# Four pairs of gate units move out of the first stage of a hybrid encoder layer and run behind it as seven block products each

## The chip, the cores and the metric

The kernel runs on one core of one Trainium2 chip. The metric is the device time of one execution in microseconds (us), the median of several runs. One further execution was taken by the hardware profiler; its rows are in us from the start of its span, with the engines named PE (matmuls), DVE (vector), ACT (scalar), POOL and SP (the engine that issues the DMAs).

## The reference

One encoder layer on 1024 tokens behind 16 meta tokens, width 1024, all in float32. One wide projection of the normed input is cut into the inputs of two branches and two gates:

```python
proj = h @ w_in[l]
(q, k, v, z, b_raw, a_raw, sc_b, sc_c, sc_x, gate_a, gate_b) = jnp.split(proj, SPLIT_POINTS, axis=-1)
o_dn = gated_deltanet_bidir(q, k, v, z, b_raw, a_raw, ...)     # times silu(z) at its end
y_a = o_dn @ w_branch_dn[l]
y_b = (sc_b * depthwise_conv_centred(sc_c * sc_x, sc_conv_w[l])) @ w_branch_sc[l]
merged = jax.nn.sigmoid(gate_a) * y_a + jax.nn.sigmoid(gate_b) * y_b
h_res = h_res + merged @ w_out[l]
gu = h2 @ w_gate_up[l]
h_res = h_res + (silu(gu[..., :D_FF]) * gu[..., D_FF:]) @ w_down[l]
```

The change concerns gate_a, gate_b (1024 columns each, 8 units of 128), z (8 units, one a head) and the short convolution y_b.

## The kernel before

Every product is done on operands that are split into a rounded high part and the low rest (`split`, L98: an ACT copy rounds, a DVE subtraction leaves the rest), as three matmuls: high·high, high·low, low·high. A unit is 128 output columns over 1024 tokens: 2 halves of 512 tokens, 8 steps of the contraction, 3 matmuls each, so 48 matmuls of 512 columns. Its weights come in one DMA of 512 KB into a raw tile (two of them take turns) and are split into `wh` and `wl` (two buffers each). PSUM has eight banks of 512 columns, under the names pm, pe and pd. The normed input lies in SBUF transposed, `hTh` its high part and `al_...` (three tiles) its low part.

**Stage 1** (up to L1393) runs the 24 q, k and v units and, between them, *fill units*: gates, z of the first five heads (`ZH = 5`), and 24 units of the short convolution, in this order (`fill_units`, L958 to 963). Gates go to DRAM as `ta_d` and `tb_d`, z as `z_d`, the convolution as `p_d` (eight tiles, stored by halves out of `rb`, L452), the heads' results as `o_d`. Beside the units four streams run for each head (decay, norm, inverse, scan), whose small matmuls are put between those of the units. The order is written by a planner at build time: it keeps a clock per engine (`T`), adds a cost for each instruction that it places (`pe`, `V`, `A`, `on`), and lets a stream go on when PE's clock has reached the time at which the stream's data should be ready. In `g_norm` a loop over the nine chunks multiplies the decay matrices PQ with products of k and q (L602, L641); `on("dve", 500)` stands ahead of it, and `freed_at` says when a bank is free again. The instructions of stage 1 stay in the planner's order on every engine.

**Behind stage 1** the framework's scheduler orders the instructions of each engine, once, at build time. A new pool takes the place of stage 1's SBUF memory, with the tiles b0 to b3 (16 KB a partition each), mA and mB, four s4, w2, and two more raw tiles. Whatever is written there first waits until stage 1's last reads of that memory are done, the stores of `p_d` among them. Then:

- the three z units left (L1411 to 1418), into mB;
- `px`: the eight `p_d` tiles are loaded into s4 tiles and split into b0 to b3 (L1422 to 1426);
- `w_bsc`: eight units on px, times tanh-form gate B, into mA and mB (`mg`); `gated(h)` (L1429) loads o_d, multiplies it by silu(z) and splits it into `ox`;
- `w_bdn`: eight units on ox, times gate A, added; then w_out with the residual and the second norm;
- the feed-forward part: 22 units of two weight blocks of 128 columns each (L1561 is their matmul), and the down projection.

The feed-forward part uses seven block products instead of eight. With weights A11, A12 (one unit's two halves of the contraction), A21, A22 (the other's), and the moving operand's blocks B (halves of the contraction by halves of the tokens), it forms S1 = A21 + A22, S3 = A11 − A21, S2 = S1 − A11, S4 = A12 − S2 (`sums`, L1535) and T1 = B12 − B11, T2 = B22 − T1, T3 = B22 − B12, T4 = B21 − T2 once, and multiplies A11·B11, A12·B21, S2·T2, S1·T1, S3·T3, S4·B22, A22·T4. A product (`product`, L1555) is 4 steps × 3 = 12 matmuls, so a pair takes 84 where two units take 96.

Of the kernel before, what the change touches and what calls it, by code (L numbers as in the profile page):

```python
# [28 lines left out]
ZH = 5  # L29
EPS = 1e-6  # L30
NEG = -1e30

OQ, OK, OV, OZ, OBA, OSB, OSC, OSX, OGA, OGB = (
    0, 1024, 2048, 3072, 4096, 4128, 5152, 6176, 7200, 8224)


def unit(col):

    return (col if col < OBA else col - 32) // P
# [8 lines left out]
def encoder_layer(ctx: ExitStack, tc: tile.TileContext, x, meta, norm1_w, w_in, w_ba,  # L48
                  dn_conv_w, A_log, dt_bias, dn_norm_w, sc_conv_w, w_bdn, w_bsc,
                  w_out, norm2_w, w_gu, w_down, final_w, out):  # L50
    nc = tc.nc
    x, out = x[0], out[0]
# [7 lines left out]
    dr = ctx.enter_context(tc.tile_pool(name="dr", bufs=1, space=DRAM))  # L60
# [16 lines left out]
    def pss():  # L77
        return ps.tile([P, 512], F32, tag="d", name=uid("pd"), bufs=3)
# [3 lines left out]
    def psz():  # L82

        rot["i"] += 1
        return (psm, psd, psm, psd, psd)[rot["i"] % 5]()
# [8 lines left out]
    mm = nc.tensor.matmul  # L94
# [4 lines left out]
    def split(hi, lo, src):  # L99
        nc.scalar.copy(hi, src)  # L100
        nc.vector.tensor_tensor(out=lo, in0=src, in1=hi.bitcast(F32), op=ALU.subtract)  # L101
# [75 lines left out]
    def sub(out, a, b):  # L177
        nc.vector.tensor_tensor(out=out, in0=a, in1=b, op=ALU.subtract)
# [67 lines left out]
    low_tiles = low([LP])  # L246
# [18 lines left out]
    def on(e, ns, ready=0.0):  # L265

        T[e] = max(T[e], ready, T["pe"]) + ns
        return T[e] + TOPE
# [5 lines left out]
    def V(n, kind=0):  # L274
        return on("dve", (68 + 1.042 * n, 130 + 1.042 * n, 130 + 0.52 * n)[kind])
# [210 lines left out]
    B = lambda b: slice(32 * b, 32 * b + 32)  # L486
# [62 lines left out]
    def g_norm(h, st_):  # L549
# [79 lines left out]
        for c in range(NC):  # L629
            while not nxt or c not in st_["exp"]:  # L630
                ask()
                yield T["pe"] + 100
            pk, t = nxt.pop(0)
            while T["pe"] < max(t, st_["exp"][c]):
                ask()
                yield T["pe"] + 100
            for d in range(2):
                nc.vector.scalar_tensor_tensor(out=NP[:, c, d], in0=pk[:, 0:P], scalar=cc[:, c, d:d + 1],
                                               in1=PQ[:, c, d], op0=ALU.mult, op1=ALU.mult)
                V(P, 1)  # L640
            nc.vector.tensor_tensor(out=PQ[:, c], in0=pk[:, P:2 * P].unsqueeze(1).broadcast_to([P, 2, P]), in1=PQ[:, c],  # L641
                                    op=ALU.mult)
# [140 lines left out]
    def g_scan(h, st_):  # L783
# [159 lines left out]
        for c4 in range(2):  # L943
            oT = NP[:, 4 * c4:4 * c4 + 4, 1 - c4]
            pt = newbank()
            for c in range(4):
# [452 lines left out]
    def big(tag, shape, dtype=F32R):  # L1399
        return tp.tile(shape, dtype, tag=tag, name=uid(tag))  # L1400

    def four(tag):

        tiles = [big(f"b{i}", [P, 4, SEQ]) for i in range(4)]
        return [[tiles[2 * i + k // 4][:, k % 4] for k in range(KT)] for i in range(2)]

    px = four("p")
    mg = [big("mA", [P, 4, SEQ], F32), big("mB", [P, 4, SEQ], F32)]
    szs = {}
    for h in range(ZH, H):  # L1410
        w = wload(w_in, unit(OZ + h * P))  # L1411
        sz = szs[h] = mg[1][:, h - ZH]
        for i in range(2):
            po = psany()
            dense(po, w, hx, C0 + META + 512 * i, 512)
            sl = slice(512 * i, 512 * i + 512)
            nc.scalar.activation(sz[:, sl], po, AF.Tanh, scale=0.5)
            nc.vector.scalar_tensor_tensor(out=sz[:, sl], in0=sz[:, sl], scalar=1.0, in1=po, op0=ALU.add, op1=ALU.mult)

    warm2 = keep.tile([P, 1], F32, name="warm2")  # L1420
    nc.scalar.activation(warm2, szs[H - 1][:, SEQ - 1:SEQ], AF.Silu)
    for j in range(KT):  # L1422
        pr = s4(SEQ)
        nc.sync.dma_start(pr, p_d[j])
        split(px[0][j], px[1][j], pr)
    raw_slots.extend((tp, f"raw{i}") for i in range(2))
    ox = (ap_.tile([P, KT, SEQ], F32R, tag="ah", name="oh"), eighths(low([SEQ])))

    def gated(h):  # L1429

        ot = s4(SEQ)
        nc.sync.dma_start(ot, o_d[h])
        if h not in szs:
            szs[h] = s4(SEQ)
            nc.sync.dma_start(szs[h], z_d[h])
        nc.vector.scalar_tensor_tensor(out=ot, in0=ot, scalar=cols[:, 24:25], in1=szs[h], op0=ALU.mult, op1=ALU.mult)
        split(ox[0][:, h], ox[1][h], ot)

    gated_order = [*range(ZH, H), *range(ZH)]
    for j in range(KT):  # L1440
        w = wload(w_bsc, j)
        if j == 0:
            for h in range(ZH, H):
                gated(gated_order.pop(0))
# [78 lines left out]
    def stationary1(j):  # L1523
# [11 lines left out]
    def sums(rg, ru, s2, s4_, s3, s1):  # L1535
        g0, g1, u0, u1 = rg[:, 0:4], rg[:, 4:8], ru[:, 0:4], ru[:, 4:8]
        nc.vector.tensor_tensor(out=s1, in0=u0, in1=u1, op=ALU.add)
        sub(s3, g0, u0)
        sub(s2, s1, g0)
        sub(s4_, g1, s2)  # L1540

    def stationary2(j, ru, sa, sb, A_):

        for i, r in enumerate((sa, sb)):
            sh, sl = (s_hl[j % 2][:, m, i] for m in range(2))
            split(sh, sl, r)
            for x, n in enumerate((("S2", "S4"), ("S3", "S1"))[i]):
                A_[n] = sh[:, 4 * x:4 * x + 4], sl[:, 4 * x:4 * x + 4]

    def block22(j, ru, A_):  # L1550
        uh, ul = (u_hl[j % 2][:, i] for i in range(2))
        split(uh, ul, ru[:, 4:8])
        A_["A22"] = uh, ul

    def product(po, a, b, add_to=False):  # L1555

        (ah, al), (bh, bl) = a, mov[b]
        for k in range(4):
            bhk, blk = (m[k] if isinstance(m, list) else m[:, k] for m in (bh, bl))
            for x, y, i in ((ah, bhk, 0), (ah, blk, 1), (al, bhk, 2)):  # L1560
                mm(po, x[:, k], y, start=k + i == 0 and not add_to, stop=k == 3 and i == 2, skip_group_check=add_to)  # L1561

    add = lambda out, a, b: nc.vector.tensor_tensor(out=out, in0=a, in1=b, op=ALU.add)  # L1563
    mul = lambda out, a, b: nc.vector.tensor_tensor(out=out, in0=a, in1=b, op=ALU.mult)

    def part1(w, p1, sg):

# [253 lines left out]
```

## Time and profile before

| | us |
|---|---|
| median of 3 runs (2011.54 to 2012.34) | 2011.95 |
| the profiled execution | 2009.93 |
| its span | 2008.2 |
| mean granted clock of PE | 0.997 |
| PE, DVE, ACT, POOL busy | 1988.4, 1341.5, 815.6, 108.6 |
| last matmul of stage 1 ends, about | 1062.4 |
| first matmul of w_bsc | 1095.05 |

How to read it: in the rows, "out<-in" are the tiles written and read by the program's names, x the number of instructions, and in brackets the idle time of the engine before the row with what ended it. A row of a wait list gives the total, the number and the longest. A back-to-back matmul shows 0.39 us although the next starts 0.227 us later, since their ends overlap; the distance of starts is the pace.

### The profile page before, as it was taken

The page shows a single profiled execution, that of the slowest core. Times are in us where ns is not written, and L with a number is a line of the kernel's source. Part 1 is how long each engine was busy: PE and PEld are TensorE (multiplying, and loading weights), DVE is VectorE, ACT ScalarE, POOL GpSimd, SP SyncE. Part 2 cuts the span into 40 slices and gives each one's busy share as a digit, 9 for nine tenths or more (in the row PEclk, how much of TensorE's full clock was granted, in tenths as well). Part 3 has the DMA queues.
Part 4 walks back from the last instruction along what each step waited for, and adds up shares of the span by engine and source line. Part 5 has one row for each costly group of instructions (what it writes and reads, how often), then busy time and mean ns, then how long its engine had stood idle before and what let it go on. Part 6 is the DMA issues. An engine that isn't in the chain of part 4 may idle for free.

```text
span 2008.2 us, 31913 instructions
## 1 busy us (share of the span) xinstructions
PE 1988.4 (99%) x12059; PEld 1730.0 (86%) x12059; DVE 1341.5 (67%) x2966; ACT 815.6 (41%) x1945; POOL 108.6 (5%) x407
## 2 busy tenths in 40 slices
PE   9999999999999999999999999999999999999998
PEld 8998889898989899999998888887888888888887
DVE  6887687887888788845335434468866666646575
ACT  6463464646555536333113211224423333334344
POOL 2011101010101020100000000000000000000000
PEclk9999999999999999999999999999999999999999
DMA  3122222323222212221216633122666345477654
GB/s 134 64 90 87 87 90 61 104 69 91 69 80 74 69 57 72 59 75 53 73 54 241 216 130 116 50 98 101 245 225 222 137 150 187 159 271 244 195 172 167
DMA packets 131409, 247.85 MB, mean 123 GB/s; under 512 B 45045, under 2 KB 54694, under 8 KB 128823
## 3 DMA queue, kind: packets, MB, share of 16 engines
q1 hardware_dynamic: 130679, 244.77, 36.9%
q8 instruction: 94, 1.54, 0.3%
q10 hardware_dynamic: 576, 1.05, 0.1%
q14 instruction: 60, 0.49, 0.1%
HBM read 179.10 MB, written 66.67 MB: 122 GB/s over the span
## 4 chain that ended last, share of the span: by engine, by line
PE 90%; DVE 5%; ACT 2%; DMA 2%; issue 1%; SPq 0%; POOL 0%; DVEq 0%; ACTq 0%; POOLq 0%
PE pm L340 35%; PE pd L1561 11%; PE pe L1561 5%; PE pm L1561 3%; PE pe L133 1%; PE pe L135 1%; PE pe L134 1%; PE pd L901 1%; PE pe L602 1%; PE pd L133 1%; PE pd L135 1%; PE pd L134 1%; PE pd L880 1%; PE pe L1728 1%; PE pe L1727 1%; PE pe L1729 1%
## 5 line engine op out<-in xcount | busy, mean ns | idle before, releaser
L340 PE MATMUL pm<-hTh,wh 128*128 128x512 f32 (+4 forms) x1424 | 496.6, 353 | 0.4 <-ACT hTh L1101 0.2
L340 PE MATMUL pm<-al,wh 128*128 128x512 f32 (+4 forms) x1424 | 495.1, 352 | 0.0
L340 PE MATMUL pm<-hTh,wl 128*128 128x512 f32 (+4 forms) x1424 | 494.5, 352 | 0.0
L340 PEld LDWEIGHTS pm<-hTh,wh 128*128 128x128 f32 x1424 | 267.0, 188 | 18.0 <-ACT hTh L1101 0.8
L340 PEld LDWEIGHTS pm<-hTh,wl 128*128 128x128 f32 x1424 | 267.1, 188 | 17.1 <-issue 0.8
L340 PEld LDWEIGHTS pm<-al,wh 128*128 128x128 f32 x1424 | 267.1, 188 | 16.5 <-issue 0.4
L101 DVE TENSOR_TENSOR al<-raw,ring_h 128x1024 fp32r<-128x1024 f32 x73 | 88.5, 1221 | 65.6 <-ACT ring_h L100 64.8
L988 DVE TENSOR_TENSOR wl<-raw,wh 128x512 fp32r<-128x512 f32 x134 | 90.6, 687 | 58.2 <-ACT wh L991 57.9
L100 ACT CAST ring_h<-raw 128x1024 fp32r<-128x1024 f32 x73 | 76.7, 1053 | 107.0 <-PE pd L1729 33.9
L362 DVE SCALAR_TENSOR_TENSOR kq<-ra,wc,kq 128x520 f32<-128x520 f32 x128 | 96.5, 754 | 6.2 <-ACT kq L392 5.3
L991 ACT CAST wh<-raw 128x512 fp32r<-128x512 f32 x134 | 79.5, 621 | 30.4 <-PE pm L340 26.7
L100 ACT CAST wh<-raw 128x1024 fp32r<-128x1024 f32 x43 | 45.1, 1050 | 99.2 <-PE pe L134 35.3
L887 ACT ACTIVATE w<-pd,small 128x128 f32<-128x128 f32 x128 | 39.9, 364 | 100.7 <-PE pd L880 100.4
L495 DVE TENSOR_TENSOR tm<-fP,fN 128x135 f32<-128x135 f32 (+23 forms) x248 | 71.9, 290 | 4.6 <-DVE fP L499 0.2
L499 DVE TENSOR_TENSOR fP<-fP,tm 128x135 f32<-128x135 f32 (+23 forms) x248 | 71.2, 287 | 4.9
L1563 DVE TENSOR_TENSOR b<-pd,b 128x512 f32<-128x512 f32 x22 | 15.2, 690 | 68.9 <-PE pd L1561 68.9
L1664 ACT ACTIVATE b<-b 128x512 f32<-128x512 f32 x22 | 13.9, 632 | 112.8 <-DVE b L1563 112.8
L101 DVE TENSOR_TENSOR wl<-raw,wh 128x1024 fp32r<-128x1024 f32 x43 | 52.4, 1218 | 4.9 <-ACT wh L100 4.8
L1561 PE MATMUL pd<-b_hl,wh 128*128 128x512 f32 x176 | 54.4, 390 | 0.0
L854 ACT ACTIVATE jk<-NP 128x128 f32<-128x128 f32 x64 | 19.9, 311 | 82.6 <-DVE NP L850 81.5
L545 ACT ACTIVATE PQ<-PQ,negG 128x128 f32<-128x128 f32 x128 | 43.6, 394 | 20.2 <-DVE PQ L540 20.1
L874 DVE SCALAR_TENSOR_TENSOR r<-pd,negEG,vS 128x128 f32<-128x128 f32 x120 | 36.7, 345 | 21.8 <-PE pd L864 21.5
(523 smaller groups left out, 4419.5 us busy)
## 6 DMA issues: line engine op xcount, KB each, us to landing
raw<-in_w_in_dram SPq DMA_DIRECT2D x72, 512.0 KB
raw<-in_w_gate_up_dram SPq DMA_DIRECT2D x44, 512.0 KB
sums<-in_w_down_dram SPq DMA_DIRECT2D x22, 512.0 KB
t_d<-sums SPq DMA_DIRECT2D x11, 1024.0 KB
raw<-s_d SPq DMA_DIRECT2D x44, 256.0 KB
raw<-t_d SPq DMA_DIRECT2D x44, 256.0 KB
act_d<-b SPq DMA_DIRECT2D x43, 256.0 KB
raw<-act_d SPq DMA_DIRECT2D x33, 256.0 KB
```

Of the source, the lines that this page charges most:

```text
L100: nc.scalar.copy(hi, src)
L101: nc.vector.tensor_tensor(out=lo, in0=src, in1=hi.bitcast(F32), op=ALU.subtract)
L133: mm(po[:m, :n], wh[:, k, :m], xhk[:, t0:t0 + n], start=(k == 0), stop=False)
L134: mm(po[:m, :n], wh[:, k, :m], xlk[:, t0:t0 + n], start=False, stop=False)
L340: mm(po[:, :n], ww[:, k], f(k)[:, t0:t0 + n], start=i == 0, stop=i == 3 * KT - 1)
L362: nc.vector.scalar_tensor_tensor(out=acc, in0=raw[:, h0 + t:h0 + t + hn], scalar=wc[:, t, col:col + 1], in1=acc, op0=ALU.mult, op1=ALU.add)
L495: nc.vector.tensor_tensor(out=tv, in0=fP[:, 0:r, j:j + 1].broadcast_to([P, r, n]), in1=fN[:, j:j + 1, j + 1:32].broadcast_to([P, r, n]), o ...
L499: nc.vector.tensor_tensor(out=fP[:, 0:r, j + 1:32], in0=fP[:, 0:r, j + 1:32], in1=tv, op=ALU.subtract)
L545: nc.scalar.activation(PQ[:, c, d], PQ[:, c, d], AF.Exp, bias=negG2[:, c, hd:hd + 1])
L988: nc.vector.tensor_tensor(out=u[1][1][:, k], in0=u[2][:, k], in1=u[1][0][:, k].bitcast(F32), op=ALU.subtract)
L991: nc.scalar.copy(u[1][0][:, k], u[2][:, k])
L1561: mm(po, x[:, k], y, start=k + i == 0 and not add_to, stop=k == 3 and i == 2, skip_group_check=add_to)
```

## The change

`GH = 4`: only gates 0 to 3 stay fill units; the eight units of gates 4 to 7 are made by four calls of `pair(n, j)` behind the z units, each with gate A and gate B of one j as its two units, in seven products. For these `moving_sums()` forms T1 to T4 of the normed input into b0 to b3, with mA and mB as scratch (all passes on DVE but the rounding). z of heads 5 to 7 goes to DRAM like the others and is loaded again in `gated`, which takes one head a step from head 0. `px` comes behind the pairs, with `mg`: p_d 0 to 3 are loaded into mA, 4 and 5 into s4 tiles, 6 and 7 into raw tiles. In the planner, 900 instead of 500 is added to DVE's clock ahead of the decay loop, and each chunk gets 110 more and a bank that counts as free 100 later. `sums`, `stationary2`, `product` and the two short helpers move up unchanged. In all PE has 48 matmuls of 512 columns less.

```diff
+GH = 4
-    z_d = [dr.tile([P, SEQ], F32, name=f"z_d{i}") for i in range(ZH)]
+    z_d = [dr.tile([P, SEQ], F32, name=f"z_d{i}") for i in range(H)]
-        on("dve", 500)
+        on("dve", 900)
-            freed_at.append(V(2 * P))
+            on("dve", 110)
+            freed_at.append(V(2 * P) + 100)
-                   for j in range(8) for off, d_ in ((OGA, ta_d), (OGB, tb_d))]
+                   for j in range(GH) for off, d_ in ((OGA, ta_d), (OGB, tb_d))]
-    px = four("p")
-    mg = [big("mA", [P, 4, SEQ], F32), big("mB", [P, 4, SEQ], F32)]
-    szs = {}
+    def moving_sums():
+
+        c = [slice(C0 + META + 512 * i, C0 + META + 512 * i + 512) for i in range(2)]
...
+        x, y = (big(g, [P, 2, 4, 512], F32) for g in ("mA", "mB"))
+        t1, t2, t3, d_ = x[:, 0], x[:, 1], y[:, 0], y[:, 1]
+        a, b = slice(0, 2), slice(2, 4)
+        sub(t1, h0[1], h0[0])
+        sub(d_, l0[1], l0[0])
+        add(t1, t1, d_)
+        split(*mov["T1"], t1)
+        sub(t2, h1[1], t1)
...
+        split(*mov["T4"], t1)
+
+    raw_slots.extend((tp, f"raw{i}") for i in range(2))
+    weights_z = [wload(w_in, unit(OZ + ZH * P))]
+    moving_sums()
     for h in range(ZH, H):
-        w = wload(w_in, unit(OZ + h * P))
-        sz = szs[h] = mg[1][:, h - ZH]
+        w = weights_z.pop() if weights_z else wload(w_in, unit(OZ + h * P))
+        sz = s4(SEQ)
...
+        nc.sync.dma_start(z_d[h], sz)
+    def pair(n, j):
+
+        last = j == KT - 1
+        s_hl[n % 2] = big(("mB", "mA")[n % 2], [P, 2, 2, KT, P])
...
+        if not last:
+            product(bank, A_["S2"], "T2", True)
+            nc.scalar.copy(o1[:, right], bank)
+            product(bank2, A_["S1"], "T1")
+            nc.scalar.copy(o2[:, right], bank2)
+            product(bank, A_["S3"], "T3", True)
...
+            product(bank2, A_["S4"], "B22", True)
+            add(o1[:, right], bank2, o1[:, right])
+            half_turn(o1[:, right])
+        nc.sync.dma_start(ta_d[j], o1)
+        nc.sync.dma_start(tb_d[j], o2)
+        return o1
+
+    for n, j in enumerate(range(GH, KT)):
+        o1 = pair(n, j)
-    nc.scalar.activation(warm2, szs[H - 1][:, SEQ - 1:SEQ], AF.Silu)
+    nc.scalar.activation(warm2, o1[:, SEQ - 1:SEQ], AF.Silu)
+    mg = [big("mA", [P, 4, SEQ], F32), big("mB", [P, 4, SEQ], F32)]
+    px = four("p")
     for j in range(KT):
-        pr = s4(SEQ)
+        pr = mg[0][:, j] if j < 4 else s4(SEQ) if j < 6 else rawtile([P, SEQ])
         nc.sync.dma_start(pr, p_d[j])
         split(px[0][j], px[1][j], pr)
-    raw_slots.extend((tp, f"raw{i}") for i in range(2))
-        if h not in szs:
-            szs[h] = s4(SEQ)
-            nc.sync.dma_start(szs[h], z_d[h])
+        sz = s4(SEQ)
+        nc.sync.dma_start(sz, z_d[h])
```

What the scheduler makes of it, at three places (numbers of tiles are running numbers; a row is one instruction, or several where an x stands).

DVE before, from the end of stage 1: the last short-conv rows (rb), the low part of the second z unit's weights (wl_12903), px splits (b), the third's (wl_12963).

```order
L450 TENSOR_TENSOR rb_12781<-pm_12802,rb_12781 128x512
L101 TENSOR_TENSOR wl_12903<-raw_12904,wh_12902 128x1024
L1418 SCALAR_TENSOR_TENSOR mB_12841<-mB_12841,pm_12848 128x512
L101 TENSOR_TENSOR b_2143_12838<-s_2162_13024,b_2141_12836 128x1024
L101 TENSOR_TENSOR b_2143_12838<-s_2163_13028,b_2141_12836 128x1024
L101 TENSOR_TENSOR b_2143_12838<-s_2164_13032,b_2141_12836 128x1024
L1418 SCALAR_TENSOR_TENSOR mB_12841<-mB_12841,pe_12875 128x512
L101 TENSOR_TENSOR wl_12963<-raw_12964,wh_12962 128x1024
```

DVE after, at the same place: the low part of the second z unit's weights is wl_12417, then come the T sums in mA and mB and their low parts in b.

```order
L451 TENSOR_TENSOR rb_12272<-pm_12293,rb_12272 128x512
L102 TENSOR_TENSOR wl_12417<-raw_12418,wh_12416 128x1024
L179 TENSOR_TENSOR mA_12337<-hTh 128x2048
L179 TENSOR_TENSOR mB_12338<-al_124 128x2048
L179 TENSOR_TENSOR mB_12338<-hTh 128x2048
L1409 TENSOR_TENSOR mA_12337<-mA_12337,mB_12338 128x2048
L1486 SCALAR_TENSOR_TENSOR s_2094_12360<-s_2094_12360,pm_12361 128x512
L179 TENSOR_TENSOR mA_12337<-hTh,mA_12337 128x2048
L102 TENSOR_TENSOR b_2088_12333<-mA_12337,b_2088_12333 128x2048
L1409 TENSOR_TENSOR mA_12337<-mA_12337,al_125 128x1024
L1409 TENSOR_TENSOR mA_12337<-mA_12337,al_126 128x1024
```

And the end of that piece, behind three rows that are left out, up to the low part of the third z unit's weights (wl_12479); s_2094 and s_2100 are z tiles.

```order
L1409 TENSOR_TENSOR mB_12338<-mB_12338 128x2048
L179 TENSOR_TENSOR mA_12337<-hTh,mA_12337 128x2048
L102 TENSOR_TENSOR b_2090_12335<-mB_12338,b_2090_12335 128x2048
L1409 TENSOR_TENSOR mA_12337<-mA_12337,al_125 128x1024
L1409 TENSOR_TENSOR mA_12337<-mA_12337,al_126 128x1024
L1486 SCALAR_TENSOR_TENSOR s_2094_12360<-s_2094_12360,pe_12388 128x512
L1486 SCALAR_TENSOR_TENSOR s_2100_12422<-s_2100_12422,pe_12423 128x512
L1486 SCALAR_TENSOR_TENSOR s_2100_12422<-s_2100_12422,pe_12450 128x512
L102 TENSOR_TENSOR wl_12479<-raw_12480,wh_12478 128x1024
L102 TENSOR_TENSOR b_2091_12336<-mA_12337,b_2091_12336 128x2048
```

Between the second and the third unit's low parts lay three px passes of 1024 columns and two z passes of 512; now ten passes of 2048, six of 1024 and four of 512 stand there.

PE after, at the third z unit (wh_12478, wl_12479) and the first products of the first pair (wh_12542):

```order
L136 MATMUL pe_12450<-hTh,wl_12417 128x512
L134 MATMUL pd_12485<-hTh,wh_12478 128x512
L135 MATMUL pd_12485<-al_124,wh_12478 128x512
L134 MATMUL pd_12512<-hTh,wh_12478 128x512
L135 MATMUL pd_12512<-al_124,wh_12478 128x512
L1440 MATMUL pd_12550<-hTh,wh_12542 128x512
L1440 MATMUL pd_12550<-al_124,wh_12542 128x512
L1440 MATMUL pm_12566<-hTh,wh_12542 128x512
L1440 MATMUL pm_12566<-al_125,wh_12542 128x512
L136 MATMUL pd_12485<-hTh,wl_12479 128x512
```

Two matmuls for each half of the third z unit and four of the pair were drawn ahead of the first row that reads wl_12479.

SP before, behind the last stores of p_d: the px loads follow at once, into s4 tiles (s).

```order
L452 DMA p_d_82<-rb_12769 128x512
L452 DMA p_d_82<-rb_12781 128x512
L118 DMA raw_13062<-in_w_branch_sc_dram 128x1024
L1424 DMA s_2162_13024<-p_d_75 128x1024
L1424 DMA s_2163_13028<-p_d_76 128x1024
L1424 DMA s_2164_13032<-p_d_77 128x1024
L1424 DMA s_2165_13036<-p_d_78 128x1024
L1424 DMA s_2166_13040<-p_d_79 128x1024
```

SP after, at the px loads: s_2147 is the last pair's gate A, mA_13027 the first half of `mg` on the memory of the last pair's S blocks.

```order
L1577 DMA s_2168_13071<-o_d_107 128x1024
L119 DMA raw_13208<-in_w_branch_sc_dram 128x1024
L1579 DMA s_2169_13073<-z_d_99 128x1024
L1558 DMA tb_d_98<-s_2148_12911 128x1024
L119 DMA raw_13275<-in_w_branch_sc_dram 128x1024
L1570 DMA mA_13027<-p_d_75 128x1024
L1557 DMA ta_d_90<-s_2147_12910 128x1024
L1570 DMA mA_13027<-p_d_76 128x1024
L1570 DMA mA_13027<-p_d_77 128x1024
L1570 DMA mA_13027<-p_d_78 128x1024
```

The loads of p_d 0 to 3 (p_d_75 to 78) stand behind the pairs, and three of them behind the store of ta_d_90.

PE after, from the last pair's last product (mA_12903 are its S blocks) to the first w_bsc units (wh_13065):

```order
L1440 MATMUL pe_12925<-hTh,mA_12903 128x512
L134 MATMUL pd_13080<-b_2154_13029,wh_13065 128x512
L134 MATMUL pm_13106<-b_2154_13029,wh_13065 128x512
L135 MATMUL pd_13080<-b_2156_13031,wh_13065 128x512
L136 MATMUL pd_13080<-b_2154_13029,wl_13066 128x512
L135 MATMUL pm_13106<-b_2156_13031,wh_13065 128x512
L136 MATMUL pm_13106<-b_2154_13029,wl_13066 128x512
L134 MATMUL pm_13147<-b_2154_13029,wh_13139 128x512
L134 MATMUL pd_13080<-b_2154_13029,wh_13065 128x512
```

The first rows of w_bsc, on the high parts of p_d 0 to 3 (b_2154), now stand right behind the last row that reads mA_12903.

More of the change, by code (lines that the diff above doesn't have):

```diff
@@ L1405, in four, with sums @@
         return [[tiles[2 * i + k // 4][:, k % 4] for k in range(KT)] for i in range(2)]
-    px = four("p")
-    mg = [big("mA", [P, 4, SEQ], F32), big("mB", [P, 4, SEQ], F32)]
-    szs = {}
+    add = lambda out, a, b: nc.vector.tensor_tensor(out=out, in0=a, in1=b, op=ALU.add)
+    mul = lambda out, a, b: nc.vector.tensor_tensor(out=out, in0=a, in1=b, op=ALU.mult)
+    s_hl, u_hl = [None, None], [None, None]
+    mov = {}
+    def sums(rg, ru, s2, s4_, s3, s1):
+        g0, g1, u0, u1 = rg[:, 0:4], rg[:, 4:8], ru[:, 0:4], ru[:, 4:8]
+        nc.vector.tensor_tensor(out=s1, in0=u0, in1=u1, op=ALU.add)
+        sub(s3, g0, u0)
+        sub(s2, s1, g0)
+        sub(s4_, g1, s2)
@@ new lines, in stationary2, with block22, product @@
+    def stationary2(j, ru, sa, sb, A_):
+        for i, r in enumerate((sa, sb)):
+            sh, sl = (s_hl[j % 2][:, m, i] for m in range(2))
+            split(sh, sl, r)
+            for x, n in enumerate((("S2", "S4"), ("S3", "S1"))[i]):
+                A_[n] = sh[:, 4 * x:4 * x + 4], sl[:, 4 * x:4 * x + 4]
+    def block22(j, ru, A_):
+        uh, ul = (u_hl[j % 2][:, i] for i in range(2))
+        split(uh, ul, ru[:, 4:8])
+        A_["A22"] = uh, ul
+    def product(po, a, b, add_to=False):
+        (ah, al), (bh, bl) = a, mov[b]
+        for k in range(4):
+            bhk, blk = (m[k] if isinstance(m, list) else m[:, k] for m in (bh, bl))
+            for x, y, i in ((ah, bhk, 0), (ah, blk, 1), (al, bhk, 2)):
+                mm(po, x[:, k], y, start=k + i == 0 and not add_to, stop=k == 3 and i == 2, skip_group_check=add_to)
@@ new lines, in moving_sums @@
+    def moving_sums():
+        c = [slice(C0 + META + 512 * i, C0 + META + 512 * i + 512) for i in range(2)]
+        f = lambda m: m.bitcast(F32)
+        h0, h1 = ([f(hx[0][:, 4 * i:4 * i + 4, cc]) for cc in c] for i in range(2))
+        l0, l1, l2 = ([f(t[:, :, cc]) for cc in c] for t in low_tiles)
+        for i in range(2):
+            for j in range(2):
+                mov[f"B{i + 1}{j + 1}"] = hx[0][:, 4 * i:4 * i + 4, c[j]], [hx[1][4 * i + k][:, c[j]] for k in range(4)]
+        for i, n in enumerate(("T1", "T2", "T3", "T4")):
+            t = big(f"b{i}", [P, 2, 4, 512])
+            mov[n] = t[:, 0], t[:, 1]
+        x, y = (big(g, [P, 2, 4, 512], F32) for g in ("mA", "mB"))
[6 more added lines that the diff above has]
+        sub(t2, h1[1], t1)
+        add(t2[:, a], t2[:, a], l1[1])
+        add(t2[:, b], t2[:, b], l2[1])
+        split(*mov["T2"], t2)
+        sub(t3, h1[1], h0[1])
+        sub(d_[:, a], l1[1], l0[1][:, a])
+        sub(d_[:, b], l2[1], l0[1][:, b])
+        add(t3, t3, d_)
+        split(*mov["T3"], t3)
+        sub(t1, h1[0], t2)
+        add(t1[:, a], t1[:, a], l1[0])
+        add(t1[:, b], t1[:, b], l2[0])
+        split(*mov["T4"], t1)
@@ L1442, in encoder_layer @@
         if j == 0:
-            for h in range(ZH, H):
-                gated(gated_order.pop(0))
+            gated(gated_order.pop(0))
         tb = s4(SEQ)
@@ L1533, in stationary1 @@
         return rg, ru, {"A11": (gh[:, 0:4], gl[:, 0:4]), "A12": (gh[:, 4:8], gl[:, 4:8])}, (gh, gl)
[L1535 to L1564, printed above, removed]
     def part1(w, p1, sg):
```

58 lines of the change are left out of this document (56 added, 2 removed).

## The prediction

> **What bounds the kernel now.** I read the page first: span, busy shares, the strip of forty slices, and the summary of the chain that ended last.
>
> ```profile
> span 2008.2 us, 31913 instructions
> PE 1988.4 (99%) x12059; PEld 1730.0 (86%) x12059; DVE 1341.5 (67%) x2966; ACT 815.6 (41%) x1945; POOL 108.6 (5%) x407
> PE   9999999999999999999999999999999999999998
> PEclk9999999999999999999999999999999999999999
> PE 90%; DVE 5%; ACT 2%; DMA 2%; issue 1%; SPq 0%; POOL 0%; DVEq 0%; ACTq 0%; POOLq 0%
> ```
>
> PE is busy in every slice at an undivided clock, and 90% of the chain is PE. So a matmul taken away is worth its pace, and everything else counts only where PE has to wait for it. Next I read what PE waited for in the whole run.
>
> ```profile
> PE pd L1561 <- ACT b L100: 2.6, 1, 2.6
> PE pe L602 <- DVE PQ L641: 2.5, 2, 2.4
> PE pd L97 <- POOL eps L1759: 1.6, 1, 1.6
> ```
>
> These are the three longest, under 7 us together: one at the start of the feed-forward part (L1561), one in the decay loop (L602), one at the end. A new wait of some us would therefore stand out, and nothing in the kernel makes it up again. Third, the pace of a matmul, from the chain in time, and the stretches on which the terms below rest (columns: PE busy, weight loads, DVE, ACT, POOL, granted clock, DMA share, GB/s).
>
> ```profile
> 1417.17 2.72 PE pe L1561 x12
> 1419.89 2.72 PE pd L1561 x12
> ...
> 942.00:1062.40 120.40, 120.40 (x683) 112.77 (x682) 39.50 (x64) 16.32 (x32) 0.20 (x2) 1.00 0.21 68
> 1062.40:1095.00 32.60, 32.60 (x145) 27.02 (x144) 19.09 (x19) 13.81 (x16) 0.00 (x0) 1.00 0.83 291
> 1394.00:1402.00 8.00, 7.10 (x22) 5.09 (x23) 6.97 (x9) 2.73 (x5) 0.00 (x0) 0.79 0.46 164
> 684.00:692.00 8.00, 7.49 (x148) 6.39 (x148) 7.31 (x22) 2.48 (x7) 0.00 (x0) 0.79 0.15 60
> 1400.00:1790.00 390.00, 389.74 (x1717) 321.70 (x1716) 260.92 (x354) 137.41 (x187) 0.00 (x0) 1.00 0.56 195
> 362.00:662.00 300.00, 299.11 (x2404) 268.57 (x2403) 244.69 (x736) 164.22 (x530) 34.97 (x141) 1.00 0.25 78
> ```
>
> One product is 12 matmuls of 512 columns in 2.72 us, so one costs 2.72/12 = 0.2267 us. The stretch 942 to 1062.4 is the tail of stage 1, where nothing but fill units runs. 1062.4 to 1095 is the three z units (144 matmuls × 0.2267 = 32.6), with px prepared beside them and no idle PE.
>
> **The change part by part.** Times below count from t = 0, the end of stage 1's last matmul.
>
> *Fewer matmuls: −10.9 us.* Eight gate units of 48 matmuls leave stage 1 (384 × 0.2267 = 87.0 us) and return as four pairs of 7 × 12 = 84. Each pair saves 12: 48 × 0.2267 = 10.9. Moving 336 matmuls is worth nothing by itself, because PE is full on both sides. The feed-forward stretch 1400 to 1790 runs the same form of product with PE busy 389.74 of 390.00, with its own sums and splits beside it; I take the pairs at that pace once they run.
>
> *The T sums ahead of the third z unit's weights: +12.4 us.* In the new DVE order ten passes of 128x2048, six of 128x1024 and four of 128x512 stand between the second z unit's low part and the third's (wl_12479). DVE works in order. The prices:
>
> ```profile
> 1382.20 4.48 DVE L101 TENSOR_TENSOR b<-al,b 128x2048 fp32r<-128x2048 f32 x2
> ...
> 1078.25 3.49 DVE L101 TENSOR_TENSOR b<-s,b 128x1024 fp32r<-128x1024 f32 x3
> ...
> 1076.52 0.68 DVE L1418 SCALAR_TENSOR_TENSOR mB<-mB,pe 128x512 f32<-128x512 f32 x1
> 1077.11 1.22 DVE L101 TENSOR_TENSOR wl<-raw,wh 128x1024 fp32r<-128x1024 f32 x1
> ```
>
> Back to back that is 4.48/2 = 2.24, 3.49/3 = 1.16 and 1077.11 − 1076.52 = 0.59 us. The queue is 10 × 2.24 + 6 × 1.16 + 4 × 0.59 = 31.7 us, and the low part itself 1.2. When can it begin? Its first pass writes mA, on stage 1's memory, and must wait until the last short-conv rows have been stored.
>
> ```profile
> 1062.41 0.39 PE L133 MATMUL pm<-hTh,wh 128*128 128x512 f32 x1
> ...
> 1065.48 11.46 SPq L1424 DMA_DIRECT2D s<-p_d  x7
> ```
>
> Before, stage 1 ended at 1062.41, and the first load that needs the same stores was issued at 1065.48: t = 3.1. So wl_12479 is whole at 3.1 + 31.7 + 1.2 = 36.0. Until then PE has two z units and eight matmuls that were drawn forward: (96 + 8) × 0.2267 = 23.6. It stands idle for 12.4 us. ACT's rounding casts keep just ahead (1.9 us each for 2048 columns, below) and should add nothing. Bounds: 10, if DVE starts at t = 1 and some passes are shorter, to 15, if a cast or a store is late twice. Behind this the pairs' own weight sums stand in the same queue; DVE gains on PE from there, since a pair asks for 84 × 0.2267 = 19.0 us of PE and the feed-forward stretch keeps DVE at 260.92/390.00 = 67% for the same kind of work.
>
> *px behind the pairs: +6.5 us.* Before, the eight p_d loads and splits lay beside the z units. Now p_d 0 to 3 go into mA, which holds the last pair's S blocks, and its last product (S4B22) reads them to the end of the pairs, call it E. Loads 2 to 4 stand on SP's queue behind the store of ta_d[7], which waits for the last eviction (about E + 2.2, an add and a tanh as below). What a p_d load then costs:
>
> ```profile
> 1070.26 1.05 ACT L100 CAST b<-s 128x1024 fp32r<-128x1024 f32 x1 [1.56 <-DMA s<-p_d]
> 1071.75 1.05 ACT L100 CAST b<-s 128x1024 fp32r<-128x1024 f32 x1 [0.43 <-DMA s<-p_d]
> 1074.29 1.05 ACT L100 CAST b<-s 128x1024 fp32r<-128x1024 f32 x1 [1.49 <-DMA s<-p_d]
> ...
> 1082.25 1.22 DVE L101 TENSOR_TENSOR b<-s,b 128x1024 fp32r<-128x1024 f32 x1
> ...
> 1098.47 1.28 ACT L1421 ACT_TABLE_LOAD   x1
> ...
> 1392.33 1.90 ACT L100 CAST b<-al 128x2048 fp32r<-128x2048 f32 x1 [5.46 <-DVE al L227]
> 1394.28 0.50 PE L1561 MATMUL pd<-b,w 128*128 128x512 f32 x1 [2.60 <-ACT b L100]
> ```
>
> The load issued at 1065.48 was cast at 1070.26, 4.8 us later, and the next two 1.5 and 2.5 us after that. So the first cast begins about E + 4.8 (behind the activation table's 1.28 us, hidden by then), its low part is done 1.05 + 1.22 later at E + 7.1, and the fourth, issued from E + 2.7, about E + 12 to 14. Meanwhile PE can run the blocks of p_d 4 to 7 only: 26 matmuls stand in its order before it is bound to the late four, 26 × 0.2267 = 5.9 us. The wait is 12.4 − 5.9 = 6.5 us, between 5 and 8 by the same rows (landing 1.5 us earlier or later).
>
> *The clock behind each idle time: +3.0 us.* After the waits of 2.4 and 2.6 us the granted clock over the next 8 us is 0.79 (rows 684 and 1394 above), a price of 0.21 × 8 = 1.7 us. Two new waits make 3.4; in px part of it is hidden under the remaining waits, so I take 3.0, from 0 (all hidden) to 5 (a wait in several pieces). The Trainium skill, page "TensorE: Matmul & The Clock Gate", section "HAM oscillation — how this bites in real kernels", gives a rule: "no PE-idle gaps >~3.4µs". By it the waits of 2.4 and 2.6 us should not have touched the clock; the rows 684 and 1394 show 0.79 behind both, so the measurement decides, and by the rule only the decay wait's part of the next term would be smaller by 1.7 us.
>
> *Stage 1: −2.0 us.* The larger numbers in the decay loop only move matmuls: L602 is asked for later, so that its wait can vanish.
>
> ```profile
> 681.79 0.34 PE L340 MATMUL pm<-hTh,wl 128*128 128x384 f32 x1
> 684.51 0.67 PE L602 MATMUL pe<-kq 128*128 128x256 f32 x2 [2.38 <-DVE PQ L641]
> ```
>
> That is worth 2.5 us and its 1.7 of clock: 4.2 at best. Against it, the short-conv units now run inside the head streams instead of in the pure tail (683 fill matmuls stood behind the last scan, 99 now), and DVE is already 244.69/300 = 82% busy from 362 to 662, where PE nevertheless lost under 1 us. One or two more waits like that of 681.8 would cost 4.2 each. Between −4.2 and +5 I take −2.0, nearer to the row that shows how little a full DVE has cost.
>
> *z 5 to 7 through DRAM, reordered gating:* nothing; three stores and three loads more of 512 KB, before stages with a DMA share of 0.56 to 0.83 that PE did not notice. Without that cover one late load would cost about the 4.8 us above.
>
> **Sum:** −10.9 + 12.4 + 6.5 + 3.0 − 2.0 = +9.0 us. The profiled execution took 2009.93 us (span 2008.2), so it would come to 2018.9. The median of the runs before, 2011.95, lies 2.0 above, so the forecast is 2021 us. About 0.2%, 4 us, is what a measurement of this kernel can tell from no change.
>
> **The rivals.**
> - *The low part of the third z unit comes in time* (other side). If DVE ran the T passes in the gaps of stage 1's tail, or the load of the weights let it go first, the queue ahead of it would be under 23.6 − 3.1 − 1.2 = 19.3 us instead of 31.7, and the 12.4 and 1.7 go: 2021 − 14.1 = 2006.9. For it: DVE is only 39.50/120.40 busy in the tail. Against it: the order of the queue is fixed, and mA is not free before the stores. With px hidden as well it would be about 1998.7. Chance 0.13.
> - *Only half of it.* One wait is a good deal smaller, or stage 1 gains its 4.2 and px waits 5 with no clock loss: 2021 − 6 to 8 = about 2014, within no change. Chance 0.17.
> - *The fuller streams run dry.* With shorts inside the streams DVE comes late at L602 or in the scans, two or three times at 4.2 us: 2021 + 2 + 8.4 = about 2031. For it: DVE at 82%. Against it: under 1 us lost there in 300. Chance 0.10.
> - *The change does not save what it says.* The pairs' products read a bank that is still being added to by the last one and so wait about one product each, 4 × 2.72 = 10.9, which eats the whole saving: 2032. Against it: the feed-forward stretch with the same chain of products waits nowhere. Chance 0.05.
>
> **How the numbers follow.** The forecast, both waits within their bounds, has 0.55 (about 2014 to 2028). Faster (under 2007.9): the first rival less its upper edge, and a little of the second, 0.13. Same (2007.9 to 2016.0): the second rival, the first's edge and the forecast's lower one, 0.20. Slower: the rest, 0.67. The range of 8 in 10 takes in the lower rivals down to 2007 and the bounds upwards, 2.6 for the first wait, 1.5 for the second, 2 for the clock and 3 of the 7 of stage 1, 2021 + 9.1 = 2030: 2007 to 2030.
>
> **What would show it.** Right: PE idle 10 to 15 us about 24 us behind stage 1's last matmul, ended by DVE's low part of a z weight; a second idle time of 5 to 8 us in the first w_bsc unit, ended by a low part of p_d; clock below 0.9 behind both; PE without waits between the pairs' products; 48 matmuls fewer; the wait of L602 gone or small. Wrong: if the third z unit starts without a wait the first rival holds; if waits at L602 or in the scans add up to over 5 us, the third; if PE waits inside the pairs, the fourth.

## The result and the profile after

The changed kernel takes 2020.68 us (median of 6 runs, 2018.89 to 2023.88), the kernel before 2011.6 us (median of 6 runs beside it, 2009.31 to 2012.34). The ratio is 1.0053, 95% interval 1.0043 to 1.0063; it is an estimate of its own and not the quotient of the two medians, which is 1.0045. So the change makes the kernel slower, by 9.1 us between the medians and by 10.7 by the ratio, where 9.0 had been forecast (2021).

The page of the profiled execution, with the strips that stood full before:

```profile
span 2022.2 us, 31878 instructions
PE 1980.3 (98%) x12011; PEld 1724.5 (85%) x12011; DVE 1398.3 (69%) x3013; ACT 838.1 (41%) x1961; POOL 109.2 (5%) x407
PE   9999999999999999999798999999999999999998
PEclk9999999999999999999899999999999999999999
PE 88%; DVE 6%; DMA 3%; ACT 2%; issue 1%; SPq 0%; DVEq 0%; ACTq 0%
```

The count of PE instructions is down by 48 (12059 to 12011). In PE's strip two slices, 20 and 22, are no longer full, and the clock of slice 20 is down too. A slice is 2022.2/40 = 50.6 us, so these are 961 to 1011 and 1062 to 1112 us: the third z unit and the first w_bsc unit. The list of PE's waits names what ended them:

```profile
PE pd L136 <- DVE wl L102: 11.5, 1, 11.5
PE pd L134 <- ACT b L101: 6.0, 1, 6.0
PE pd L1440 <- DVE b L1409: 3.3, 2, 2.7
PE pd L1440 <- ACT b L101: 2.6, 1, 2.6
PE pe L603 <- DVE PQ L642: 1.9, 1, 1.9
```

The two at the top are new; the 2.6 is the old wait at the start of the feed-forward part; L603 stands for the old L602. PE in time, first at the z units, then at w_bsc (a row's bracket holds the idle time before it and what ended it):

```profile
970.85 0.39 PE L134 MATMUL pm<-hTh,wh 128*128 128x512 f32 x1
...
994.54 0.39 PE L1440 MATMUL pm<-al,wh 128*128 128x512 f32 x1
1006.41 0.79 PE L136 MATMUL pd<-hTh,wl 128*128 128x512 f32 x1 [11.48 <-DVE wl L102]
1007.00 0.63 PE L134 MATMUL pd<-hTh,wh 128*128 128x512 f32 x1
1007.43 0.63 PE L135 MATMUL pd<-al,wh 128*128 128x512 f32 x1
...
1012.06 0.40 PE L134 MATMUL pd<-hTh,wh 128*128 128x512 f32 x1
...
1094.32 0.39 PE L1440 MATMUL pe<-hTh,mA 128*128 128x512 f32 x1
1100.72 0.80 PE L134 MATMUL pd<-b,wh 128*128 128x512 f32 x1 [6.01 <-ACT b L101]
...
1104.22 0.40 PE L134 MATMUL pd<-b,wh 128*128 128x512 f32 x1
```

Stage 1 ends at 970.85, where 1062.4 − 87.0 = 975.4 would be the old place less the eight units: it gained 4.5 us. The first wait ends 35.6 us later. Behind it the matmuls start 0.43 us apart instead of 0.227, about half the pace: 13 of them take 1012.06 − 1006.41 = 5.65 us instead of 13 × 0.2267 = 2.95, which is 2.7 us of clock; behind the second wait 7 take 3.50 instead of 1.59, another 1.9.

This profiled execution took 2023.88 us, the longest of the six, and is 14.0 longer in span than the one before. The parts seen so far are −10.9 + 11.5 + 2.7 + 6.0 + 1.9 − 4.5 = +6.7. Another 2.7 and its clock, some 1.7, belong to a wait in the feed-forward part that the next profiles show shorter (last section); the rest, 2.9, lies at several places, none of them above 1 us.

### The profile page after: what moved, and what is told of

Same layout as the page of the kernel before. It is cut to its first block, busy times and chain, and to the rows that moved or that the text cites. A ratio compares the mean times of both kernels' runs of the same rounds, so it can differ in the third digit from the quotient of the medians.

```text
span 2022.2 us, 31878 instructions
## 1 busy us (share of the span) xinstructions
PE 1980.3 (98%) x12011; PEld 1724.5 (85%) x12011; DVE 1398.3 (69%) x3013; ACT 838.1 (41%) x1961; POOL 109.2 (5%) x407
## 4 chain that ended last, share of the span: by engine, by line
PE 88%; DVE 6%; DMA 3%; ACT 2%; issue 1%; SPq 0%; DVEq 0%; ACTq 0%
PE pm L341 32%; PE pd L1440 11%; PE pe L1440 5%; PE pm L1440 3%; PE pd L903 1%; PE pd L882 1%; PE pd L866 1%; PE pe L603 1%; PE pd L136 1%; PE pd L135 1%; PE pd L134 1%; PE pd L869 1%; PE pe L1839 1%; PE pe L1841 1%; PE pe L1840 1%; PE pd L899 1%
## 5 line engine op out<-in xcount | busy, mean ns | idle before, releaser
L341 PE MATMUL pm<-hTh,wh 128*128 128x512 f32 (+4 forms) x1296 | 446.9, 350 | 0.4 <-ACT hTh L1103 0.2
L341 PE MATMUL pm<-al,wh 128*128 128x512 f32 (+4 forms) x1296 | 446.2, 349 | 0.0
L341 PE MATMUL pm<-hTh,wl 128*128 128x512 f32 (+4 forms) x1296 | 444.1, 348 | 0.0
L341 PEld LDWEIGHTS pm<-hTh,wh 128*128 128x128 f32 x1296 | 242.9, 189 | 13.6 <-issue 0.8
L341 PEld LDWEIGHTS pm<-al,wh 128*128 128x128 f32 x1296 | 243.1, 189 | 12.4 <-issue 0.4
L341 PEld LDWEIGHTS pm<-hTh,wl 128*128 128x128 f32 x1296 | 243.1, 189 | 12.3 <-issue 0.4
L990 DVE TENSOR_TENSOR wl<-raw,wh 128x512 fp32r<-128x512 f32 x118 | 79.5, 688 | 30.6 <-ACT wh L993 30.2
L993 ACT CAST wh<-raw 128x512 fp32r<-128x512 f32 x118 | 69.2, 621 | 3.7 <-issue 3.6
L102 DVE TENSOR_TENSOR wl<-raw,wh 128x1024 fp32r<-128x1024 f32 x47 | 57.4, 1220 | 8.1 <-ACT wh L101 8.0
L912 DVE SCALAR_TENSOR_TENSOR S<-S,eGl,pd 128x128 f32<-128x128 f32 x104 | 31.6, 342 | 30.4 <-PE pd L899 30.0
```

Of the source, the lines that this page charges most:

```text
L341: mm(po[:, :n], ww[:, k], f(k)[:, t0:t0 + n], start=i == 0, stop=i == 3 * KT - 1)
L912: nc.vector.scalar_tensor_tensor(out=Sn, in0=S[d], scalar=eGl[:, cd[d], hd[d]:hd[d] + 1], in1=b1[:, d], op0=ALU.mult, op1=ALU.add)
L990: nc.vector.tensor_tensor(out=u[1][1][:, k], in0=u[2][:, k], in1=u[1][0][:, k].bitcast(F32), op=ALU.subtract)
L993: nc.scalar.copy(u[1][0][:, k], u[2][:, k])
```

## The experiments

Each kernel was timed against the kernel before on the same chip, where that one took 2009.6 (first four) and 2010.0 us (the others); ratios are to it. The expectations count from 2011.6, so their times stand some 2 us higher than what these chips show. Differences to the changed kernel are taken between ratios; between medians they are 1 to 2 us smaller. "The version with both waits removed" is the fourth.

**The third z unit's weights ahead of most T sums.**

```diff
-    moving_sums()
     for h in range(ZH, H):
         w = weights_z.pop() if weights_z else wload(w_in, unit(OZ + h * P))
+        if h == H - 1:
+            moving_sums()
```

> The changed kernel with one thing moved: the T sums are written behind the third z unit's weight load, so that its low part stands in DVE's queue after four passes of 2048 columns instead of ten. My theory (PE waits for what stands last in DVE's queue): the 11.5 us wait for this low part goes, but all the T sums still stand ahead of the first pair's low part, which comes at about 3.1 + 36.3 + 1.2 = 40.6 us behind stage 1, while PE has 150 matmuls = 34.0 us: a wait of 6 to 8 us at the first pair's first low part, and about 2 of clock behind it. Total 4 to 5 us below the changed kernel's 2020.7, about 2016. Rival (the T sums cost nothing but this one low part): the whole 14.7 us go, 2006. Rival (PE waits for something else, such as memory of stage 1): no change, 2020.7.

Measured: 2015.08 us, ratio 1.0024 (1.0013 to 1.0034), so 5.8 us less than the changed kernel (1.0053 − 1.0024 = 0.0029 of 2010). PE's longest waits in it, then PE at the first pair:

```profile
PE pd L134 <- ACT b L101: 6.1, 1, 6.1
PE pd L1440 <- DVE s L1487: 5.5, 1, 5.5
```

```profile
1009.96 0.76 PE L1440 MATMUL pd<-hTh,wh 128*128 128x512 f32 x1 [5.49 <-DVE s L1487]
...
1011.60 0.80 PE L1440 MATMUL pd<-hTh,wl 128*128 128x512 f32 x1 [0.45 <-DVE wl L102]
```

The wait at the third z unit is gone and stands at the first pair now, as forecast, a little shorter (5.49 + 0.45 us), ended first by a z pass (the bank that a pair's matmul wants) and then by the pair's low part, which is the next row on DVE. So the T sums as a whole are late, not one row among them; and the third z unit did not wait for memory.

**p_d into the other buffer.**

```diff
-        pr = mg[0][:, j] if j < 4 else s4(SEQ) if j < 6 else rawtile([P, SEQ])
+        pr = mg[1][:, j] if j < 4 else s4(SEQ) if j < 6 else rawtile([P, SEQ])
```

> The changed kernel with p_d 0 to 3 loaded into mB instead of mA; mB is free a whole pair (19 us) earlier, since the last pair's S blocks lie in mA. My theory (px is late because its buffer is): the 6.0 us wait at the first w_bsc unit goes and the half clock behind it (1.9), about 2012.8, within 1. Rival (the loads are late because the queues are full and the T tiles, which px overwrites, are read until the end): the wait stays above 4 us, about 2019 to 2021.

Measured: 2010.19 us, ratio 1.0003 (0.9994 to 1.0011): 10.0 us less than the changed kernel (8.5 between the medians), where the wait and the half clock of its profile make 7.9. SP, ACT and PE of this run:

```profile
1074.48 2.15 SPq L1570 DMA_DIRECT2D mB<-p_d  x2
...
1081.76 3.90 ACT L101 CAST b<-mB 128x1024 fp32r<-128x1024 f32 x4 [1.18 <-PE pe L1440]
...
1092.35 0.39 PE L1440 MATMUL pe<-hTh,mA 128*128 128x512 f32 x1
1092.57 0.39 PE L134 MATMUL pd<-b,wh 128*128 128x512 f32 x1
```

The last of the four loads is issued by 1076.6, 16 us ahead of the pairs' end; the casts wait for PE to finish with the T tiles, not for a load; and w_bsc starts 0.22 us behind the last pair. The T tiles do hold the casts back, but these begin some 11 us ahead of PE's need. The rival (full queues, T tiles read to the end) is out as the cause of the wait: it was the buffer.

**T sums in pieces, two heads first.** The generator form of `moving_sums` yields behind T1, T2 and T3; the heads of pairs 0 and 1 (the products that need no T) run ahead of the rest.

```diff
+    t_sums = moving_sums()
+    next(t_sums)
     for h in range(ZH, H):
         w = weights_z.pop() if weights_z else wload(w_in, unit(OZ + h * P))
+        if h == H - 1:
+            next(t_sums)
...
+    first = gate_weights(GH)
+    split(first[0], first[1], first[2])
+    next(t_sums)
...
+    pairs = [pair(n, j) for n, j in enumerate(range(GH, KT))]
+    for p in pairs[:2]:
+        next(p)
```

> The changed kernel with the T sums cut into four pieces that stand between the weights as PE needs them, and with the products A11 B11 and A12 B21 of the first two pairs, which need no T, ahead of the others; the same instructions otherwise. My theory: DVE has 3.1 + 34.7 = 37.8 us of work up to the second pair's low part and 42.7 up to the first S block, PE 38.5 and 43.5, so no wait is left but perhaps 1 to 2 us at the second S block; 14.7 less, 2006 to 2008. Rival (this stage is bound by DVE's or the DMA's total work and the wait only moves on): a wait of 5 us or more shows up inside the pairs, 2013 or more.

Measured: 2005.78 us, ratio 0.9983 (0.9974 to 0.9992): 14.1 us less than the changed kernel. Its longest waits:

```profile
PE pd L134 <- ACT b L101: 5.8, 1, 5.8
PE pd L1440 <- ACT b L101: 2.6, 1, 2.6
```

What is left is the wait at px and the old one. Inside the pairs no wait is above 0.45 us. The same instructions in another order, on DVE and, with the two heads moved forward, on PE, take the 11.5 us and their clock away. So it was the order, not the stage's total of DVE work.

**Both.**

> Both changes of the two runs before together. My theory (the two waits are separate): the gains add, 14 and 8, so 1998 to 2000, clearly below the kernel before (2011.6) by about 12 us: the 10.9 of the matmuls saved and the gain in stage 1. Rival (what is won at the first is lost at the second, since both stand behind the same DVE queue): 2006 or more.

Measured: 1996.83 us, ratio 0.9935 (0.9922 to 0.9949): 23.7 us less than the changed kernel and about 13 less than the kernel before, faster than both. The gains of the two runs add, within the intervals: 14.1 + 10.0 = 24.1. PE is as good as full in the stretch of the z units and pairs (the columns as in the prediction):

```profile
970.00:1090.00 120.00, 119.55 (x527) 98.33 (x526) 88.48 (x85) 55.63 (x69) 0.00 (x0) 1.00 0.47 166
```

**The planner's numbers alone**, in the kernel before:

```diff
-        on("dve", 500)
+        on("dve", 900)
-            freed_at.append(V(2 * P))
+            on("dve", 110)
+            freed_at.append(V(2 * P) + 100)
```

> The kernel before with the planner's three new numbers alone (900, 110, 100). My theory: the wait of 2.4 us at L602 and the half clock behind it go, 2 to 4.2 us less than the kernel before, and stage 1 ends 2 to 4 us earlier than at 1062.4. Rival (the numbers do nothing and stage 1's gain of 4.5 us in the changed kernel comes from the units that left it): within 1 us of the kernel before.

Measured: 2012.72 us, ratio 1.0011 (1.0002 to 1.0020), no gain. My theory fell: the wait of 681.8 is gone, and four others stand at the same line, 4.8 us together. The list of its waits, and the first row behind stage 1:

```profile
PE pe L602 <- DVE PQ L641: 4.8, 4, 2.0
```

```profile
1063.30 0.39 PE L133 MATMUL pm<-hTh,wh 128*128 128x512 f32 x1
```

**The old numbers** in the changed kernel: the diff above the other way round, and one number more. A further `on("dve", 900)`, in `g_gates` (L1308), stands in the kernel before and in the changed one alike, and this run has 500 there too. So it is not a clean way back.

> The changed kernel with the planner's old numbers (500, nothing, nothing). My theory: stage 1 ends 2 to 4 us later than at 970.9 and so does the kernel, about 10 to 13 us above the kernel before, with a wait at L602 of 2 us or more. Rival (the units that left made the gain): as the changed kernel, about 9 above before.

Measured: 2022.81 us, ratio 1.0063 (1.0050 to 1.0075), not to be told from the changed kernel's 1.0053 with certainty. Stage 1 ends 2.3 us later, as my theory had it, and both new waits are there unchanged:

```profile
973.18 0.39 PE L134 MATMUL pm<-hTh,wh 128*128 128x512 f32 x1
```

```profile
PE pd L136 <- DVE wl L102: 11.5, 1, 11.5
PE pd L134 <- ACT b L101: 6.1, 1, 6.1
PE pe L603 <- DVE PQ L642: 3.1, 2, 2.3
```

Against 975.4 this is a gain of 2.2 with the units gone and the numbers old; 4.5 with both; −0.9 (1063.30 against 1062.41) with the numbers alone. So the numbers seem to have no price of their own: they help in one order of the units and not in the other. That is not shown cleanly, since the run with the old numbers changed the one in `g_gates` as well. How much of the 4.5 would show in a median stays open.

**Plain units instead of pairs**, behind stage 1.

```diff
-    moving_sums()
...
-    for n, j in enumerate(range(GH, KT)):
-        o1 = pair(n, j)
+    for j in range(GH, KT):
+        for off, dst in ((OGA, ta_d[j]), (OGB, tb_d[j])):
+            w = wload(w_in, unit(off + j * P))
+            o1 = s4(SEQ)
+            for i in range(2):
+                po = psany()
+                dense(po, w, hx, C0 + META + 512 * i, 512)
+                nc.scalar.activation(o1[:, 512 * i:512 * i + 512], po, AF.Tanh, scale=0.5)
+            nc.sync.dma_start(dst, o1)
...
-        pr = mg[0][:, j] if j < 4 else s4(SEQ) if j < 6 else rawtile([P, SEQ])
+        pr = mg[1][:, j] if j < 4 else s4(SEQ) if j < 6 else rawtile([P, SEQ])
```

> The changed kernel with the eight gate units behind stage 1 as plain units of 48 matmuls each instead of pairs: no T sums, no S sums, 48 matmuls more, and p_d 0 to 3 loaded into mB. It shows what moving alone does. My theory (moving is worth nothing, PE is full on both sides, and each product saved is worth its matmuls): no new wait, 10.9 us above the version with both waits removed less its last wait of 0.7, that is about 2 to 4 below the kernel before. Rival (gates behind stage 1 leave the streams without cover, or make new waits): the kernel before or above. Rival (the seven products do not save their 10.9 us): within 3 us of the version with both waits removed.

Measured: 2005.91 us, ratio 0.9978 (0.9969 to 0.9987), 4 below the kernel before and 8.7 above the version with both waits removed (0.9978 − 0.9935 = 0.0043). With the widths of the two intervals, some 3 us, that agrees with the 10.2 that the matmul count gives. The profiles show it without the noise of the medians. The first row behind stage 1 and the first of w_bsc, with plain units and then with both waits removed:

```profile
969.31 0.39 PE L134 MATMUL pm<-hTh,wh 128*128 128x512 f32 x1
...
1088.99 0.39 PE L134 MATMUL pd<-b,wh 128*128 128x512 f32 x1
```

```profile
970.15 0.39 PE L134 MATMUL pm<-hTh,wh 128*128 128x512 f32 x1
...
1079.95 0.39 PE L134 MATMUL pd<-b,wh 128*128 128x512 f32 x1
```

The stretch is 119.7 us with plain units and 109.8 with pairs, 9.9 less. Moving alone is worth stage 1's gain and no more; the seven products are worth about their matmuls.

**Five pairs** (`GH = 3` in the third experiment's kernel):

> The version with the T sums in pieces and two heads first, with GH = 3: five pairs instead of four, so that the last pair's S blocks lie in mB and the p_d loads into mA find it free a pair earlier without an edit. 12 matmuls less again, and 96 fill matmuls less in stage 1, where 99 stood behind the last scan. My theory: the tail of fill units just covers it, 2.7 us less than the version with both waits removed, about 12.8 + 2.7 = 15.5 below the kernel before. Rival (the streams need the fill that leaves): new waits in stage 1's last 100 us, at or above the version with both waits removed.

Measured: 2012.46 us, ratio 1.0013 (1.0004 to 1.0021), 15.7 above the version with both waits removed, although it has 12 matmuls less. The rival's sign was right, its place wrong: stage 1's last fill matmul is as early as hoped, the waits come afterwards. PE's end of stage 1 and first long wait, and DVE at the first T pass:

```profile
946.57 0.39 PE L341 MATMUL pm<-hTh,wl 128*128 128x512 f32 x1
...
998.08 0.80 PE L1440 MATMUL pd<-hTh,wl 128*128 128x512 f32 x1 [3.60 <-DVE wl L102]
...
1008.42 0.70 PE L1440 MATMUL pe<-b,mB 128*128 128x512 f32 x2 [2.62 <-issue]
```

```profile
968.19 2.29 DVE L179 TENSOR_TENSOR mA<-hTh 128x2048 f32<-128x2048 f32 x1 [3.60 <-DMA o_d<-NP]
```

And the first T pass of the version with both waits removed, whose stage 1 ended at 970.15:

```profile
973.20 2.29 DVE L179 TENSOR_TENSOR mA<-hTh 128x2048 f32<-128x2048 f32 x1 [0.77 <-DMA p_d<-rb]
```

There the T sums begin 3.05 us behind the last fill matmul, once p_d has been stored. With five pairs they begin 968.19 − 946.80 = 21.4 us behind it, once the last head's result has been stored: the last scan outlives the fill units, and its memory is mA's. Everything on DVE behind it is 18 us late. PE's waits of 1.1, 3.6 and 1.0 us behind it are ended by DVE; for the one of 2.6 the profile shows no releaser.

## Why the prediction was right

The two waits came where they had been forecast, for the reasons that had been given but for one step at px (below). That the total came within 0.1 us is luck: the terms as measured in the profile are −10.9 + 11.5 + 6.0 + 4.6 − 4.5 = +6.7 instead of +9.0, and what brings the medians back to 9.1 are places outside the sum.

- *Fewer matmuls, −10.9.* The count fell by 48. Plain units against pairs measured 8.7 in the medians and 9.9 in the profiles. Right.
- *T sums ahead of the third z unit's weights, +12.4.* Measured 11.5, ended by the row that was named. DVE of the changed kernel, first and last of the queue:

```profile
973.91 2.29 DVE L179 TENSOR_TENSOR mA<-hTh 128x2048 f32<-128x2048 f32 x1 [0.77 <-DMA p_d<-rb]
...
1003.34 1.88 DVE L1486 SCALAR_TENSOR_TENSOR s<-s,pe 128x512 f32<-128x512 f32 x3
1005.14 1.22 DVE L102 TENSOR_TENSOR wl<-raw,wh 128x1024 fp32r<-128x1024 f32 x1
```

  The queue began at 973.91 − 970.85 = 3.06 us (forecast 3.1), took 1005.14 − 973.91 = 31.2 (forecast 31.7), and the low part was whole at 35.5 (forecast 36.0). This half us is about half of the miss of 0.9: a slot of 2.24 or 1.16 holds a share of the last pass's end, which overlaps the next row, while the starts in this queue lie 2.20, 1.14 and 0.60 us apart, and 10 × 2.20 + 6 × 1.14 + 4 × 0.60 = 31.2. The other half: PE's last matmul ahead of the wait ends at 994.54 + 0.39 = 994.93, t = 24.1, not 23.6, since a matmul's end that no other overlaps counts in full.
- *px behind the pairs, +6.5.* Measured 6.0, in the right unit, but ended by ACT's high part, not by a low part. The step that failed is "PE can run the blocks of p_d 4 to 7 only: 26 matmuls stand in its order before it is bound to the late four": the first of these rows reads p_d 0's high part, so PE stood at once, until the first cast was done. The later parts were hidden instead. ACT and DVE at this place:

```profile
1099.62 1.04 ACT L101 CAST b<-mA 128x1024 fp32r<-128x1024 f32 x1 [0.89 <-DMA mA<-p_d]
...
1104.83 2.50 DVE L102 TENSOR_TENSOR b<-mA,b 128x1024 fp32r<-128x1024 f32 x2 [0.28 <-ACT b L101]
```

  The first cast begins 1099.62 − 1094.55 = 5.1 us behind the last pair (forecast 4.8) and the fourth low part ends at 12.8 (forecast 12 to 14). PE began at 6.2, when that cast was done (1099.62 + 1.04 = 1100.66). By the prediction's count of 26 matmuls, and with the half clock, it had 5.9 + 1.9 us of work before it needed the last part, until about 14.0, so that part was no wait. That 6.0 lies so near 6.5 is luck: the one is a load and a cast, 5.1 + 1.0, the other the last low part less 26 matmuls, 12.4 − 5.9.
- *Clock, +3.0.* Mis-sized: 2.7 + 1.9 = 4.6, within its bounds of 0 to 5. The half clock lasts 5.65 us behind the long wait, where a loss of 1.7 us meant 3.4.
- *Stage 1, −2.0.* 4.5 in the profile, just beyond the good end of the bounds (−4.2). The step behind it failed: the wait did not vanish. In the changed kernel L603 waits 1.9 us near 288, with half clock behind it, and PE is idle in stage 1 as long as it was. Stage 1 before and after (PE busy is the second number):

```profile
0.00:1062.41 1062.41, 1054.19 (x7919) 958.41 (x7920) 764.39 (x2160) 492.49 (x1529) 108.64 (x407) 1.00 0.25 77
```

```profile
0.00:970.85 970.85, 962.23 (x7535) 886.57 (x7536) 752.41 (x2144) 476.53 (x1497) 109.17 (x407) 1.00 0.24 75
```

  That is 8.2 us idle before and 8.6 after. The larger numbers alone gain nothing in the kernel before. Where the 4.5 us come from stays open.
- *z through DRAM: nothing.* Right: with px in time w_bsc takes 1166.99 − 1079.95 = 87.0 us (the version with both waits removed), as before, 1182.09 − 1095.05.
- *No waits inside the pairs.* Right: none above 0.45 us, in the changed kernel or with the T sums in pieces.
- The rivals: the low part that comes in time was not the case, but the third experiment made it so, and its gain of 14.1 us (12.9 between the medians) is what that rival had priced, 14.1. Fuller streams did not run dry with 99 fill matmuls behind the last scan; with 96 fewer stage 1 gave its memory back too late. The pairs' products did not wait for their banks. Of the three old waits named in the prediction, the third (1.6 us) stands at the start of the run, not at its end; no term rests on it.

## What to carry to other kernels

On a kernel that is bound by one engine, a saving in its work is safe only if everything that the new form prepares on the other engines is ready in time: here 10.9 us of matmuls were saved and 22 us of waiting and half clock made, by the place of the T sums in DVE's queue and by the choice of one buffer. Count, for each engine, what stands ahead of the row that the bound engine wants next, from the moment its first buffer is free; and when cover is taken from a stage's end, ask which of its memory is freed last.

## What the runs showed of the hardware

The clock does not follow from the length of a wait alone. In the decay loop the changed kernel, the version with both waits removed and the one with only the first removed all wait 1.9 us at L603 near 288 us. The stretch of 12 us there, in the version with both waits removed, has a clock of 0.86:

```profile
283.00:295.00 12.00, 10.12 (x162) 7.34 (x162) 11.07 (x30) 5.86 (x15) 0.00 (x0) 0.86 0.07 25
```

With only the first removed, and the same wait of 1.9 us, it is undivided:

```profile
283.00:295.00 12.00, 9.77 (x168) 7.30 (x170) 11.04 (x30) 6.23 (x16) 0.42 (x2) 1.00 0.02 5
```

The Trainium skill, page "TensorE: Matmul & The Clock Gate", section "HAM oscillation — how this bites in real kernels", puts the border at idle gaps above about 3.4 us. These rows show a gap of 1.9 us with half clock behind it and one without, so that border does not hold here; what decides between them, no run here shows.

The wait in the feed-forward part begins with a load for which DVE waits. DVE of the changed kernel, and of the kernel before at the same place of the program:

```profile
1511.16 2.14 DVE L179 TENSOR_TENSOR sums<-sums 128x512 f32<-128x512 f32 x3 [5.10 <-DMA sums<-in_w_down_dram]
```

```profile
1498.68 2.15 DVE L178 TENSOR_TENSOR sums<-sums 128x512 f32<-128x512 f32 x3 [4.09 <-DMA sums<-in_w_down_dram]
```

DVE waited in both. What differs is its place against PE's twelve matmuls there, which start at 1508.38 in the changed kernel and at 1498.61 before: DVE's sums begin 2.78 us behind that start and 0.07. The last such load was issued 1.7 us later against it (1504.13, and 1492.66 before) and was 1.0 us longer under way to DVE's start (7.0 and 6.0). That is the 2.7 us by which PE waited. The change leaves the instructions of this part as they were, and in the profile with both waits removed the longest such wait of PE was 0.7. One profile of each kernel can't show how often it comes; since the profiled execution of the changed kernel lies 3.2 us above its median, it seems to belong to single executions, and that is a reason to compare medians.
